# A second norm with two up units on token halves, its chain in a new order, and output products between the last scores

## The chip, the cores and the metric

The kernel runs on one core of a Trainium2 chip. The core has a matrix engine (TensorE, PE in the profile; its weight loads are listed apart as PEld), a vector engine (VectorE, DVE), a scalar engine (ScalarE, ACT), a general engine (GpSimd, POOL) and a synchronising engine (SyncE, SP) that here issues most of the loads. Each engine works through its own instruction list in order; they wait for each other by semaphores. The metric is the time of one execution on the device in microseconds (us); less is better.

## The reference

One decoder layer on 512 tokens of 1024 channels, in float32. The parts that matter here:

```python
# mixer: an mLSTM head group and a convolution group, one output projection
mix = jnp.concatenate([h, y], axis=-1) @ w_out[l]        # (512, 2048) @ (2048, 1024)
x = x + g1 * rms_norm(mix, mix_post_g[l])

# feed-forward with the second norm ahead of it
u = rms_norm(x, ffn_pre_g[l]) * (1.0 + sc2) + sh2
up = causal_dwconv(u @ ffn_up[l], ffn_conv_w[l], ffn_conv_b[l])   # (512, 1024) @ (1024, 5632)
a, gt = jnp.split(up, 2, axis=-1)
f = (jax.nn.silu(gt) * a) @ ffn_down[l]
x = x + g2 * rms_norm(f, ffn_post_g[l])
```

`h` is the output of four mLSTM heads, each with causal scores between positions, done here in 128-position chunks; `y` is the output of the convolution group. `sc2`, `sh2`, `g1` and `g2` come from a conditioning vector through one more projection.

## The kernel before

All large products are done with float32 split in two parts: `w_split` (L185) makes a high part (ScalarE, rounded to the matrix engine's fp32r type) and a low part (source minus high part, on GpSimd unless the caller names VectorE), and `mm3` (L207) adds three products: high x high, high x low, low x high. `w_load` (L195) takes a raw buffer (two in all), issues the load of up to 2048 columns on SyncE, and splits it in four pieces of 512 columns, eight tiles. Split weights lie in a pool of 20 tiles (`wpool`), most other 128x512 tiles in a pool of 36 (`slots`).

The order on TensorE and SyncE is that of the program, written by hand. For the other engines a planner chooses: it walks through a simulated time, and each engine takes from what is ready the instruction that stands first in the program. Within the block `with in_order():` (L75, used from L1026 on) those three engines keep the program's order among the block's own instructions; instructions from outside the block can still be placed between them.

**The last head and the output projection, first half.** `attention(H - 1)` (L536) is a generator: its first two steps are the scores of two chunks each (TensorE, tile `s`, L544, scaled by VectorE, L545), the others the products with the values and the head's norm. Between the steps the program puts `mix_first(n)` (L735): for the n-th of 16 channel groups and all four token tiles (128 tokens each), three products of 512 columns into the four banks `mixa`, which hold the left half of the projection's output. The right half, `mixb`, follows from L936 on: the first 8 channel groups for all four token tiles together, the last 8 per token tile in `mix_last(tt, a, b)` (L994).

**The second norm.** Per token tile of 128 tokens there is a chain of steps:

- `chain_sums` (L955): sum of squares of the tile's `mixb` bank on ScalarE, the product with the gain row `g1r` on VectorE (`un`, L961), and `token_factor` (L714): a tiny VectorE instruction and a power on GpSimd.
- `chain_x` (L964): the new residual `x` (VectorE, L968, two halves of 512 columns), its squares (ScalarE), the product with the row `gs2r` (VectorE, L971), another factor.
- `chain_u` (L974): `un` times the factor plus the row `sh2r` (VectorE, L976).
- `turn_tile` (L980): eight 128x128 transposes on TensorE (`xT`, L984) into two banks of the pair `at`.
- `turn_out` (L986): high part on ScalarE (`u2h`, L991), low part on VectorE (`u2l`, L992).

The results lie in `u2h` and `u2l`, sorted by token half (tiles 0 and 1, tiles 2 and 3). The feed-forward's up projection has 22 units of 256 output channels (two banks each); a unit's weights are one raw block. `up_half(th, i)` (L1012) computes a unit for one token half with products of 256 columns, so it can start when two token tiles are ready. The first `NE = 3` units are done so; from unit 3 on a product takes all 512 columns (L1139). Unit 0's block is split by `w_load` with VectorE for the low parts; units 1 and 2 have their splits (`up_split`, L1005, VectorE for the low parts) at written places in the chain. The rows `gs2r` and `sh2r` go through DRAM: `send_rows` (L682) transposes the gains on TensorE and stores them, `row` (L691) reads them back to all partitions.

Of the kernel before, what the change touches and what calls it, by code (L numbers as in the profile page):

```python
# [20 lines left out]
KT = D // P  # L21
# [34 lines left out]
def decoder_layer(ctx, tc, w_glu0, x, c, adaT, vecs, w_glu, w_qko, w_v0, w_vo, w_out, w_up, w_down, out):  # L56
# [138 lines left out]
    def w_load(view, name, pool=None, tag="w", eng=None):  # L195

        n = view.shape[1]
        r = raws.tile([P, 2048], F32, tag="raw", name=name)
        nc.sync.dma_start(r[:, :n], view)
        return [w_split(r[:, a : min(a + T, n)], f"{name}_{a}", pool, tag, eng) for a in range(0, n, T)]  # L200
# [481 lines left out]
    def send_rows(a, n, queue=nc.scalar):  # L682

        ps = mmbank(f"gT{a}") if a == KT else atbank(f"gT{a}")
        PE.transpose(ps[:n, :P], gains[:, a : a + n], ident)
        t = (side if a == 3 * KT else slot)(f"gTs{a}")[:, :P]
        V.tensor_copy(t[:n, :], ps[:n, :P])
        for i in range(n // KT):
            queue.dma_start(rows_d[a // KT + i].rearrange("(j p) -> j p", p=P), t[i * KT : (i + 1) * KT, :])
# [24 lines left out]
    def token_factor(sq, name):  # L714

        t = small.tile([P, 1], F32, tag="tt", name=f"{name}t")
        last_factor[0] = V.tensor_scalar(out=t, in0=sq[:, :1], scalar1=sq[:, 1:2], scalar2=D * EPS, op0=ALU.add, op1=ALU.add)
        r = small.tile([P, 1], F32, tag="tr", name=f"{name}r")
        G.tensor_tensor(out=r, in0=t, in1=mhalf[:, :1], op=ALU.pow)
        return r  # L720
# [4 lines left out]
    KA = 8  # L725
# [9 lines left out]
    def mix_first(n):  # L735
        if n % 4 == 0:
            wo[0] = wo_rows(0, n // 4)
        k = MIX[n]
        for tt, ps in enumerate(mixa):
            mm3(ps, (hy[k][0][:, tok(tt)], hy[k][1][:, tok(tt)]), wo[0][n % 4], n == 0, n == 2 * KT - 1)  # L740
# [150 lines left out]
    tc.cur_priority -= LATER  # L891
    wo = {}
    steps = attention(H - 1)
    next(steps)
    mix_first(0)
    next(steps)
    tc.cur_priority += LATER
    for i in range(20, 24):
# [3 lines left out]
    tc.cur_priority -= LATER  # L902
    norm_rows()
    norm_tiles(0, 4)
    mix_first(1)
    mix_first(2)
    mix_first(3)
    mix_first(4)
# [46 lines left out]
    def chain_sums(tt):  # L955

        ps = banks[tt]
        sq_sum(ps, msq[:, 2 * tt + 1 : 2 * tt + 2], f"mixb{tt}")
        un = adas.tile([P, D], F32, tag="ada", name=f"un{tt}")
        uns[tt] = [un[:, :T], un[:, T:]]  # L960
        V.tensor_tensor(out=uns[tt][1], in0=ps, in1=g1r[1], op=ALU.mult)  # L961
        return token_factor(msq[:, 2 * tt : 2 * tt + 2], f"rm{tt}")

    def chain_x(tt, r):  # L964

# [8 lines left out]
    def chain_u(tt, r):  # L974
        for hf, un in enumerate(uns[tt]):
            V.scalar_tensor_tensor(out=un, in0=un, scalar=r, in1=sh2r[hf], op0=ALU.mult, op1=ALU.add)  # L976
# [3 lines left out]
    def turn_tile(tt):  # L980
        turned[tt] = [atbank(f"xT{tt}_{hf}") for hf in range(2)]
        for tp, un in zip(turned[tt], uns[tt]):
            for i in range(NT):
                PE.transpose(tp[:, i * P : (i + 1) * P], un[:, i * P : (i + 1) * P], ident)  # L984

    def turn_out(tt):  # L986
        for hf, tp in enumerate(turned[tt]):
            js = slice(NT * hf, NT * (hf + 1))
            part = tp.rearrange("p (j t) -> p j t", j=NT)
            hi, lo = (z[:, tt // 2, js, (tt % 2) * P : (tt % 2 + 1) * P] for z in (u2h, u2l))  # L990
            S.activation(hi, part, AF.Copy)  # L991
            last_lo[0] = V.tensor_tensor(out=lo, in0=part, in1=hi.bitcast(F32), op=ALU.subtract)  # L992

    def mix_last(tt, a, b):  # L994
        for n_, k in enumerate(MIX[KA:]):
            if a <= n_ < b:
                mm3(banks[tt], (hy[k][0][:, tok(tt)], hy[k][1][:, tok(tt)]), wo[n_], False, n_ == 2 * KT - KA - 1)

    def raw_up(i):
        r = raws.tile([P, 2048], F32, tag="raw", name=f"wup{i}")  # L1000
        nc.sync.dma_start(r, w_up[i])
        up_w[i] = []
        return r

    def up_split(i, r, pool, tag):  # L1005
        q = len(up_w[i])
        up_w[i].append(w_split(r[:, q * T : (q + 1) * T], f"wup{i}_{q * T}", pool, tag, V))

    NE = 3
    early = []  # L1010

    def up_half(th, i, only=None):  # L1012
# [4 lines left out]
                mm3(ps[:, th * HT : (th + 1) * HT], blk(up_w[i], half * KT + k), (u2h[:, th, k, :], u2l[:, th, k, :]), k == 0, k == KT - 1)  # L1017

    up_w = {0: w_load(w_up[0], "wup0", slots, "t", V)}
    send_rows(KT, 2 * KT, nc.sync)  # L1020
    gs2r = row(1, cvtile, "gs2", nc.sync)
    sh2r = row(2, cvtile, "sh2", nc.sync)
    raw1 = raw_up(1)
    raw2 = raw_up(2)
    early += [[mmbank(f"up{i}_{half}") for half in range(2)] for i in range(2)]
    with in_order():  # L1026
        for tt in range(3):
            mix_last(tt, 0, 2 * KT - KA)
        r = chain_sums(0)
        r = chain_x(0, r)  # L1030
        up_split(1, raw1, slots, "t")
        chain_u(0, r)
        turn_tile(0)
        mix_last(3, 0, 7)
        r = chain_sums(1)
        up_split(1, raw1, slots, "t")
        r = chain_x(1, r)
        up_split(1, raw1, slots, "t")
        chain_u(1, r)
        turn_out(0)  # L1040
        turn_tile(1)
        mix_last(3, 7, 2 * KT - KA)
        r = chain_sums(2)
        turn_out(1)
        r = chain_x(2, r)
        up_split(1, raw1, slots, "t")
        chain_u(2, r)
        up_half(0, 0)
        turn_tile(2)
        r = chain_sums(3)  # L1050
        up_split(2, raw2, wpool, "w")
        r = chain_x(3, r)
        up_split(2, raw2, wpool, "w")
        chain_u(3, r)
        up_half(0, 1)
        up_split(2, raw2, wpool, "w")
        early.append([cvbank(f"up2_{half}") for half in range(2)])
        up_half(0, 2, 0)
        turn_tile(3)
        turn_out(2)  # L1060
        up_split(2, raw2, wpool, "w")
        turn_out(3)
    up_half(0, 2, 1)
    for i in range(NE):
        up_half(1, i)
    for tt in range(NT):
# [53 lines left out]
    for i in range(NF):  # L1120
        if i < NE:
            pa, pg = early[i]
        else:
            pieces = w_load(w_up[i], f"wup{i}")
            if i in AT:
                weight_load(AT.index(i))
            if i in (4, 8, 12, 16):
                ada_block(38 + i // 2, last_lo[0])
                ada_block(39 + i // 2, last_lo[0])
            if i == 19:  # L1130
                ada_done(40, 48)
                gain(3, 40, "ffn_post_g")
            if i == 20:
                send_rows(3 * KT, KT)
            both = []
            for half in range(2):
                ps = mmbank(f"up{i}_{half}")
                for k in range(KT):
                    mm3(halves(ps), blk(pieces, half * KT + k), (u2h[:, :, k, :], u2l[:, :, k, :]), k == 0, k == KT - 1)  # L1139
                both.append(ps)  # L1140
            pa, pg = both
        a = conv3(pa, i, f"fa{i}")
        g = conv3(pg, NF + i, f"fg{i}")
        anchor[0] = S.activation(g, g, AF.Silu)
        if i % 2 == 0:
            x_, r_, *more = side_parts(f"f{i}") if i >= AT[-1] else [slot(f"f{q}{i}") for q in "xr"]
        cs = slice(i % 2 * HT, (i % 2 + 1) * HT)
        V.tensor_tensor(out=x_[:, cs], in0=a[:, :HT], in1=g[:, :HT], op=ALU.mult)
        V.tensor_tensor(out=r_[:, cs], in0=a[:, HT:], in1=g[:, HT:], op=ALU.mult)
        if i % 2:  # L1150
            y_, q_ = more or [slot(f"f{q}{i}") for q in "yq"]
            G.tensor_tensor(out=y_[:, :HT], in0=r_[:, :HT], in1=r_[:, HT:], op=ALU.add)
            G.tensor_tensor(out=y_[:, HT:], in0=y_[:, :HT], in1=x_[:, :HT], op=ALU.subtract)
            G.tensor_tensor(out=q_[:, :HT], in0=x_[:, :HT], in1=r_[:, :HT], op=ALU.subtract)
            G.tensor_tensor(out=q_[:, HT:], in0=x_[:, HT:], in1=y_[:, HT:], op=ALU.subtract)
            home = [None, None]
            if i == NF - 1:
                ends = [adas.tile([P, D], F32R, tag="ada", name=f"f{q}{i}") for q in "xy"]
                home = [(z[:, :T], z[:, T:]) for z in ends]
            af.append(split_f(x_, f"fx{i}", i == 1, home[0]))  # L1160
            asum.append(split_f(y_, f"fy{i}", i == 1, home[1]))
            j = i // 2
            nc.scalar.dma_start(spill["s34"][:, j * T : (j + 1) * T], q_)
            nc.scalar.dma_start(spill["a22"][:, j * HT : (j + 1) * HT], r_[:, HT:])
        if i - 1 in AT:
            weight_store(AT.index(i - 1))
        if i in AT:
            weight_sums(AT.index(i))
# [196 lines left out]
```

## Time and profile before

| | |
|---|---|
| median of 3 runs | 770.94 us (770.82 to 772.68) |
| the profiled execution | 771.52 us, span 769.8 us |
| granted TensorE clock | 0.998 |
| last head's scores, start of the first | 314.9 us |
| `mix_last` of the right half | 391.4 to 414.8 us |
| first up product | 414.8 us |
| last of the four turnings | 430.7 us |

Times within the profile count from the start of its span, and belong to one execution. A row of the timeline has its start, its length, the engine, the line, the operation, the tiles written and read, and in brackets how long the engine had been idle and what ended that. Where a row stands for several instructions (x2), its length is that of them all. Matrix products overlap; their spacing is the cost, not the length of one. A window's row has the busy time of PE, PEld, DVE, ACT and POOL (instructions in brackets), the clock, the share of the DMA engines and their GB/s.

### The profile page before, as it was taken

To read this page: it belongs to the slowest core of one execution; us is meant where nothing else is said; L and a number is where in the kernel's file an instruction comes from. 1 tells how busy PE (TensorE), PEld (TensorE's weight loads), DVE (VectorE), ACT (ScalarE), POOL (GpSimd) and SP (SyncE) were. 2 spreads that over 40 slices of the span, in tenths; PEclk is the share of its full clock that TensorE was granted. 3 is DMA by queue.
4 is the path that set the end of the run, shared out by engine and by line. 5 is a ranking of instruction groups with operands and counts; after the bars stand their busy time and mean duration, and the time that the engine had idled before them with its cause. 6 is when DMAs were issued, how large, how long until landed. Compare 5 with 4: busy or idle time off the path is not lost.

```text
span 769.8 us, 10292 instructions
## 1 busy us (share of the span) xinstructions
PE 758.5 (99%) x3562; PEld 630.5 (82%) x3562; DVE 573.7 (75%) x831; ACT 408.4 (53%) x780; POOL 522.7 (68%) x432
## 2 busy tenths in 40 slices
PE   8999999999999999999999999999999999999996
PEld 6788898878788788788888998888888888888885
DVE  5669999979979696476949797675765677654548
ACT  7585438585665645573334554434445246566633
POOL 4789759795494871645611467886978786599943
PEclk9999999999999999999999999999999999999999
DMA  8973214311131250655953655856686584896273
GB/s 317 347 277 126 100 56 140 135 54 56 54 111 55 110 181 38 246 192 164 378 193 135 246 185 196 301 213 232 221 302 220 215 294 145 303 399 239 96 242 141
DMA packets 40137, 147.34 MB, mean 191 GB/s; under 512 B 3826, under 2 KB 5266, under 8 KB 30484
## 3 DMA queue, kind: packets, MB, share of 16 engines
q1 hardware_dynamic: 26372, 94.50, 34.1%
q10 hardware_dynamic: 13712, 52.18, 18.8%
q8 instruction: 28, 0.46, 0.2%
q14 instruction: 25, 0.20, 0.1%
HBM read 126.59 MB, written 20.07 MB: 191 GB/s over the span
## 4 chain that ended last, share of the span: by engine, by line
PE 91%; DMA 2%; DVE 2%; POOL 2%; issue 1%; ACT 1%; DVEq 0%; POOLq 0%; ACTq 0%
PE up L210 31%; PE qko L210 13%; PE dn L210 10%; PE vo L210 9%; PE glu L210 7%; PE mixa L210 6%; PE mixb L210 6%; PE s L544 2%; PE o L555 2%; PE glu L356 2%; PE v L210 1%; DMA p<-spill_t 1%; DMA wglu<-in_w_glu 1%; POOL wglu_0l L192 0%; PE cps L159 0%
## 5 line engine op out<-in xcount | busy, mean ns | idle before, releaser
L767 DVE SCALAR_TENSOR_TENSOR cv<-gt,cvw,cv 128x485 f32<-128x485 f32 (+23 forms) x200 | 137.1, 731 | 2.9 <-ACT cv L755 1.3
L763 POOL TENSOR_TENSOR cs<-cs,cs 128x510 f32<-128x510 f32 (+3 forms) x32 | 42.1, 1318 | 0.1
L210 PE MATMUL up<-u2l,wup_0h 128*128 128x512 f32 (+1 forms) x100 | 36.5, 365 | 0.1
L210 PE MATMUL up<-u2h,wup_0h 128*128 128x512 f32 (+1 forms) x100 | 36.5, 365 | 0.0
L210 PE MATMUL up<-u2h,wup_1024h 128*128 128x512 f32 (+1 forms) x100 | 36.4, 364 | 0.0
L210 PE MATMUL up<-u2h,wup_0l 128*128 128x512 f32 (+1 forms) x100 | 36.4, 364 | 0.0
L210 PE MATMUL up<-u2l,wup_512h 128*128 128x512 f32 (+1 forms) x100 | 36.4, 364 | 0.0
L210 PE MATMUL up<-u2h,wup_512h 128*128 128x512 f32 (+1 forms) x100 | 36.4, 364 | 0.0
L210 PE MATMUL up<-u2h,wup_1536h 128*128 128x512 f32 (+1 forms) x100 | 36.4, 364 | 0.0
L210 PE MATMUL up<-u2l,wup_1536h 128*128 128x512 f32 (+1 forms) x100 | 36.4, 364 | 0.0
L210 PE MATMUL up<-u2h,wup_1536l 128*128 128x512 f32 (+1 forms) x100 | 36.4, 364 | 0.0
L210 PE MATMUL up<-u2h,wup_512l 128*128 128x512 f32 (+1 forms) x100 | 36.4, 364 | 0.0
L210 PE MATMUL up<-u2h,wup_1024l 128*128 128x512 f32 (+1 forms) x100 | 36.4, 364 | 0.0
L210 PE MATMUL up<-u2l,wup_1024h 128*128 128x512 f32 (+1 forms) x100 | 36.3, 363 | 0.0
L176 DVE SCALAR_TENSOR_TENSOR junk<-ada,cb 128x1024 bf16<-128x1024 f32 x20 | 30.1, 1506 | 4.9 <-DMA ada<-in_adaT 4.8
L192 POOL TENSOR_TENSOR wup_0l<-wup,wup_0h 128x512 fp32r<-128x512 f32 x19 | 29.3, 1543 | 4.5 <-ACT wup_0h L191 4.5
L192 POOL TENSOR_TENSOR wup_1024l<-wup,wup_1024h 128x512 fp32r<-128x512 f32 x19 | 25.0, 1318 | 9.4 <-ACT wup_1024h L191 9.4
L192 POOL TENSOR_TENSOR wup_1536l<-wup,wup_1536h 128x512 fp32r<-128x512 f32 x19 | 27.6, 1455 | 4.7 <-ACT wup_1536h L191 4.4
L761 ACT ACTIVATE cs<-gt,cvw 128x511 f32<-128x511 f32 (+4 forms) x40 | 27.2, 712 | 6.3 <-POOL cs L763 3.8
L1099 DVE TENSOR_TENSOR b<-b 128x512 f32<-128x512 f32 x11 | 19.4, 1760 | 11.3 <-POOL b L1098 11.3
L1098 POOL TENSOR_TENSOR b<-b 128x512 f32<-128x512 f32 x11 | 14.2, 1291 | 17.3 <-DVE b L1097 17.3
L336 DVE SCALAR_TENSOR_TENSOR junk<-ada,cps 128x1024 bf16<-128x1024 f32 x16 | 19.5, 1219 | 8.3 <-ACT cb L411 4.6
(1097 smaller groups left out, 2738.5 us busy)
## 6 DMA issues: line engine op xcount, KB each, us to landing
wup<-in_w_up SPq DMA_DIRECT2D x22, 1024.0 KB, 6.0
b<-in_w_down ACTq DMA_DIRECT2D x11, 1024.0 KB, 5.1
spill_t<-b ACTq DMA_DIRECT2D x11, 1024.0 KB, 3.9
ada<-in_adaT ACTq DMA_DIRECT2D x20, 512.0 KB, 4.0
wqko<-in_w_qko SPq DMA_DIRECT2D x9, 1024.0 KB, 4.8
ada<-in_adaT SPq DMA_DIRECT2D x16, 512.0 KB, 7.2
wo<-in_w_out SPq DMA_DIRECT2D x8, 1024.0 KB, 4.8
wvo<-in_w_vo SPq DMA_DIRECT2D x6, 1024.0 KB, 4.8
```

What stands on the lines that cost most here:

```text
L176: t = V.scalar_tensor_tensor(out=junk, in0=r, scalar=1.0, in1=cb, op0=ALU.mult, op1=ALU.mult, accum_out=mod[:, i : i + 1])
L192: (eng or G).tensor_tensor(out=lo[:, :n], in0=src, in1=hi[:, :n].bitcast(F32), op=ALU.subtract)
L210: PE.matmul(ps, l, r, start=start and i == 0, stop=stop and i == 2, skip_group_check=again)
L336: V.scalar_tensor_tensor(out=junk, in0=first[k][:, i * D : (i + 1) * D], scalar=1.0, in1=cps, op0=ALU.mult, op1=ALU.mult, accum_out=part[: ...
L356: PE.matmul(ps, blk(wk, i)[a], u[k][b], start=k == 0 and p == 0, stop=k == KT - 1 and p == 1)
L544: PE.matmul(sp[:, :n], ks[d][:, cc * P : (cc + 1) * P], qs[d][:, cc * P :], start=d == 0, stop=d == 1)
L555: PE.matmul(o[:, : DH + 2], E[h][cc][:, a : a + P], vs[h][cc], start=cc == 0, stop=cc == tt)
L761: S.activation(t[:, d:], cvx[j][:, : T - d], AF.Copy, scale=w(CK - 1 - d))
L763: G.tensor_tensor(out=side[:, d:], in0=side[:, d:], in1=t[:, d:], op=ALU.add)
L767: tap = V.scalar_tensor_tensor(out=cp[:, d:], in0=cvx[j][:, : T - d], scalar=w(CK - 1 - d), in1=cp[:, d:], op0=ALU.mult, op1=ALU.add)
L1098: G.tensor_tensor(out=b12, in0=b22, in1=b12, op=ALU.subtract)
L1099: V.tensor_tensor(out=b22, in0=b22, in1=b11, op=ALU.subtract)
```

## The change

Four edits.

1. `mix_first(0)` moves ahead of the last head's first scores, and `mix_first(1)` from behind `norm_tiles(0, 4)` to between the two score steps.
2. In `chain_sums` the factor is made ahead of the product with `g1r`.
3. `NE` goes from 3 to 2: two units are computed on token halves. Unit 2's block is an ordinary `w_load` behind the block, and is computed with 512 columns like the later units. Unit 1's load is issued ahead of the rows' transfers, not behind them.
4. In the chain, three of unit 1's four splits stand ahead of tile 0's sums, and the fourth before `chain_u(0)`. The turnings of tiles 0 to 3 stand after half of tile 2's `mix_last`, after half of tile 3's, between the two halves of unit 0's first token half, and between those of unit 1's. `turn_out(0)` and `turn_out(2)` stand ahead of `chain_u(1)` and `chain_u(3)`, `turn_out(1)` between `chain_x(2)` and `chain_u(2)`.

```diff
@@ -891,8 +891,9 @@
     tc.cur_priority -= LATER
     wo = {}
     steps = attention(H - 1)
+    mix_first(0)
     next(steps)
-    mix_first(0)
+    mix_first(1)
     next(steps)
     tc.cur_priority += LATER
     for i in range(20, 24):
@@ -902,7 +903,6 @@
     tc.cur_priority -= LATER
     norm_rows()
     norm_tiles(0, 4)
-    mix_first(1)
     mix_first(2)
     mix_first(3)
     mix_first(4)
@@ -958,8 +958,9 @@
         sq_sum(ps, msq[:, 2 * tt + 1 : 2 * tt + 2], f"mixb{tt}")
         un = adas.tile([P, D], F32, tag="ada", name=f"un{tt}")
         uns[tt] = [un[:, :T], un[:, T:]]
+        r = token_factor(msq[:, 2 * tt : 2 * tt + 2], f"rm{tt}")
         V.tensor_tensor(out=uns[tt][1], in0=ps, in1=g1r[1], op=ALU.mult)
-        return token_factor(msq[:, 2 * tt : 2 * tt + 2], f"rm{tt}")
+        return r
 
     def chain_x(tt, r):
 
@@ -1006,7 +1007,7 @@
         q = len(up_w[i])
         up_w[i].append(w_split(r[:, q * T : (q + 1) * T], f"wup{i}_{q * T}", pool, tag, V))
 
-    NE = 3
+    NE = 2
     early = []
 
     def up_half(th, i, only=None):
@@ -1017,50 +1018,46 @@
                 mm3(ps[:, th * HT : (th + 1) * HT], blk(up_w[i], half * KT + k), (u2h[:, th, k, :], u2l[:, th, k, :]), k == 0, k == KT - 1)
 
     up_w = {0: w_load(w_up[0], "wup0", slots, "t", V)}
+    raw1 = raw_up(1)
     send_rows(KT, 2 * KT, nc.sync)
     gs2r = row(1, cvtile, "gs2", nc.sync)
     sh2r = row(2, cvtile, "sh2", nc.sync)
-    raw1 = raw_up(1)
-    raw2 = raw_up(2)
     early += [[mmbank(f"up{i}_{half}") for half in range(2)] for i in range(2)]
     with in_order():
-        for tt in range(3):
+        for tt in range(2):
             mix_last(tt, 0, 2 * KT - KA)
+        for _ in range(3):
+            up_split(1, raw1, slots, "t")
         r = chain_sums(0)
         r = chain_x(0, r)
         up_split(1, raw1, slots, "t")
         chain_u(0, r)
+        mix_last(2, 0, 4)
         turn_tile(0)
-        mix_last(3, 0, 7)
+        mix_last(2, 4, 2 * KT - KA)
         r = chain_sums(1)
-        up_split(1, raw1, slots, "t")
         r = chain_x(1, r)
-        up_split(1, raw1, slots, "t")
+        turn_out(0)
         chain_u(1, r)
-        turn_out(0)
+        mix_last(3, 0, 4)
         turn_tile(1)
-        mix_last(3, 7, 2 * KT - KA)
+        mix_last(3, 4, 2 * KT - KA)
         r = chain_sums(2)
+        r = chain_x(2, r)
         turn_out(1)
-        r = chain_x(2, r)
-        up_split(1, raw1, slots, "t")
         chain_u(2, r)
-        up_half(0, 0)
+        up_half(0, 0, 0)
         turn_tile(2)
+        up_half(0, 0, 1)
         r = chain_sums(3)
-        up_split(2, raw2, wpool, "w")
         r = chain_x(3, r)
-        up_split(2, raw2, wpool, "w")
+        turn_out(2)
         chain_u(3, r)
-        up_half(0, 1)
-        up_split(2, raw2, wpool, "w")
-        early.append([cvbank(f"up2_{half}") for half in range(2)])
-        up_half(0, 2, 0)
+        up_half(0, 1, 0)
         turn_tile(3)
-        turn_out(2)
-        up_split(2, raw2, wpool, "w")
         turn_out(3)
-    up_half(0, 2, 1)
+        up_half(0, 1, 1)
+    up_w[2] = w_load(w_up[2], "wup2")
     for i in range(NE):
         up_half(1, i)
     for tt in range(NT):
@@ -1121,7 +1118,7 @@
         if i < NE:
             pa, pg = early[i]
         else:
-            pieces = w_load(w_up[i], f"wup{i}")
+            pieces = up_w.get(i) or w_load(w_up[i], f"wup{i}")
             if i in AT:
                 weight_load(AT.index(i))
             if i in (4, 8, 12, 16):
```

## The prediction

> **What bounds the kernel now.** I read the page's busy times and its chain first.
>
> ```profile
> PE 758.5 (99%) x3562; PEld 630.5 (82%) x3562; DVE 573.7 (75%) x831; ACT 408.4 (53%) x780; POOL 522.7 (68%) x432
> PE 91%; DMA 2%; DVE 2%; POOL 2%; issue 1%; ACT 1%; DVEq 0%; POOLq 0%; ACTq 0%
> ```
>
> TensorE sets the time nearly everywhere, so an edit is worth only the idle time or the products that it takes from PE, and costs whatever makes PE wait. I therefore went to the two places that the diff touches: the last head's scores, and the second norm. For the first, the waits of PE and a window; for the second, the chain in order of time (start, length, engine and tile).
>
> ```profile
> PE s L544 <- DVE hl L593: 0.5, 1, 0.5
> ```
> ```profile
> 312.80:315.60 2.80, 2.35 (x18) 2.03 (x17) 1.51 (x3) 1.92 (x4) 2.80 (x3) 1.00 0.96 367
> ```
> ```profile
> 391.36 16.37 PE mixb L210 x72
> 407.73 0.87 PE xT L984 x8
> 408.60 4.80 PE mixb L210 x21
> 413.40 0.45 PE xT L984 x4
> ...
> 415.26 5.90 PE up L210 x47
> 421.16 0.87 PE xT L984 x8
> 422.03 8.63 PE up L210 x72
> 430.66 0.87 PE xT L984 x8
> 431.53 20.61 PE up L210 x170
> ```
>
> 72 output products (512 columns) take 16.37 us, 0.2274 each; 72 up products on a token half (256 columns) take 8.63, 0.1199 each. The four token tiles are transposed (xT) at 407.73, 413.40, 421.16 and 430.66: PE gives the vector engines 5.7, 7.8 and 9.5 us from one tile to the next. PE waits once here, at the first up product:
>
> ```profile
> 414.60 0.39 PE L210 MATMUL mixb<-wo_1536h,yl 128*128 128x512 f32 x1
> 414.83 0.28 PE L210 MATMUL up<-u2h,wup_0h 128*128 128x256 f32 x1
> 415.26 0.38 PE L210 MATMUL up<-u2l,wup_0h 128*128 128x256 f32 x1
> 415.48 0.28 PE L210 MATMUL up<-u2h,wup_0l 128*128 128x256 f32 x1
> ```
>
> Three products, 0.36 at that rate, should end at 415.19; the fourth comes at 415.60, so 0.41 us is lost on u2l.
>
> **The change, part by part.**
>
> *Scores.* mix_first(0) fills PE's wait before the last head's scores: its banks, weights and left sides (heads 0 and 1) are long ready, and the idle time is 2.80 - 2.35 = 0.45 us of the window above. Bounds 0 and 0.45; I take 0.45. The second score pair, norm_rows and norm_tiles come one mix_first later (12 products, 2.7 us), and their first user, mix_first(6), is four mix_first further on: nothing.
>
> *Two units on halves.* Unit 2 goes from 96 products of 256 columns (11.51 us) to 48 of 512 (10.92): 0.59 gained. [...]
>
> *Order of the chain.* Per token tile VectorE does this (tile 2; the last row is turn_out's):
>
> ```profile
> 413.51 0.68 DVE L961 TENSOR_TENSOR un<-mixb,g1r 128x512 f32<-128x512 f32 x1
> 414.11 0.21 DVE L717 TENSOR_SCALAR rm2t<-msq 128x1 f32<-128x1 f32 x1
> ...
> 415.72 0.74 DVE L968 SCALAR_TENSOR_TENSOR x<-mg,rm2r,x 128x512 f32<-128x512 f32 x1
> 416.38 0.75 DVE L968 SCALAR_TENSOR_TENSOR x<-un,rm2r,x 128x512 f32<-128x512 f32 x1
> 417.04 1.29 DVE L971 TENSOR_TENSOR un<-x,gs2r 128x512 f32<-128x512 f32 x2
> ...
> 419.42 1.41 DVE L976 SCALAR_TENSOR_TENSOR un<-un,rf2r,sh2r 128x512 f32<-128x512 f32 x2
> ...
> 428.21 1.28 DVE L992 TENSOR_TENSOR u2l<-xT,u2h 128x512 fp32r<-128x512 f32 x2
> ```
>
> 0.68 + 2 x 0.21 + 1.49 + 1.29 + 1.41 + 1.28 = 6.6 us by durations (some 0.06 less per instruction by starts: 6.1). After the change PE leaves 24 x 0.2274 + 0.87 = 6.3 us from the first turning to the second, 12 x 0.2274 + 24 x 0.1199 + 0.87 = 6.5 to the third, 48 x 0.1199 + 0.87 = 6.6 to the fourth. So the chain just keeps pace, where it had up to 3 us per tile to spare. The reserve is the one at the first turning: PE gets there at 391.36 + 60 x 0.2274 = 405.0; un of tile 0 starts at 397.66 (row below), and tile 2's way from un to the end of u (413.51 to 420.83, one split and 1.2 us of u2l in it) gives 397.7 + 7.3 - 1.2 = 403.8. That is 1.2; I count 0.9, since three splits now stand ahead of tile 0's sums. The factor put ahead of un lets POOL's power run beside un (up to 0.6 us per tile), which turning inside products uses up: turn_out(1) now stands behind chain_x(2), where it stood ahead of it. If the chain is on time, the 0.41 of the first up product goes; it is 0 otherwise. Undisturbed, the whole change is worth 0.45 + 0.59 + 0.41 = 1.45 us.
>
> *Unit 1's block ahead of the gain rows.* Its buffer comes free when the last output weights are split, and the DMA engines are idle then:
>
> ```profile
> 388.46 1.31 POOL L192 TENSOR_TENSOR wo_1536l<-wo,wo_1536h 128x512 fp32r<-128x512 f32 x1
> ```
> ```profile
> 388.50:392.00 3.50, 3.50 (x18) 2.81 (x17) 2.85 (x4) 2.18 (x4) 1.27 (x2) 1.00 0.00 0
> 402.00:404.00 2.00, 2.00 (x11) 1.65 (x10) 0.48 (x1) 1.15 (x4) 0.55 (x1) 1.00 0.96 369
> ```
> ```profile
> 397.66 0.69 DVE L961 TENSOR_TENSOR un<-mixb,g1r 128x512 f32<-128x512 f32 x1 [5.35 <-ACT mixb0junk L710]
> ```
>
> 1 MB at 369 GB/s is 2.8 us from 389.8, so it should be down before 395 (estimate), and its first three splits are over when tile 0's sum is. The rows queue behind it and come up to 2 us later than now. I cost that at nothing; bound 1.3 us, under rivals.
>
> *Unit 2's block: here the time turns.* It was split by VectorE at written places. Now it is an ordinary w_load: the low halves go to POOL, and the planner is free to place them. It is issued as soon as a raw buffer is free, on SP right behind the rows, and unit 0's buffer is free from 392.1 on:
>
> ```profile
> 391.44 0.68 DVE L192 TENSOR_TENSOR wup_1536l<-wup,wup_1536h 128x512 fp32r<-128x512 f32 x1
> ...
> 418.81 0.69 DVE L192 TENSOR_TENSOR wup_1536l<-wup,wup_1536h 128x512 fp32r<-128x512 f32 x1 [0.31 <-ACT wup_1536h L191]
> ```
> ```profile
> 395.48 0.86 SPq L1001 DMA_DIRECT2D wup<-in_w_up  x2
> 419.53 14.57 SPq L199 DMA_DIRECT2D wup<-in_w_up  x3
> ```
> ```profile
> 427.54 0.62 ACT L191 ACTIVATE wup_0h<-wup 128x512 fp32r<-128x512 f32 x1
> ...
> 431.13 1.09 ACT L991 ACTIVATE u2h<-xT 128x512 fp32r<-128x512 f32 x2 [1.41 <-PE xT L984]
> ```
>
> That is what happened before with unit 3: its buffer freed at 419.5, SP issued it at 419.53, and its splits went ahead of turn_out(3), which stands earlier in the program. So unit 2's block is issued near 397 and lands near 402, and unit 3's (buffer free after unit 1's fourth split) some 5 us later. Of the 20 weight tiles 16 hold the last products' weights: four are free, for two splits at once, and mix_last(3) frees a pair at each of its eight steps, from about 408 to 415. So some eight low halves of units 2 and 3, 1.3 us each, fall on POOL between 403 and 422, where POOL had only the powers. What such a neighbour costs:
>
> ```profile
> L1099 DVE TENSOR_TENSOR b<-b 128x512 f32<-128x512 f32 x11 | 19.4, 1760 | 11.3 <-POOL b L1098 11.3
> ```
> ```profile
> 314.76 0.15 DVE L229 TENSOR_SCALAR ry_t<-ry_s 128x4 f32<-128x4 f32 x1
> ```
> ```profile
> 314.85 1.27 POOL L192 TENSOR_TENSOR wo_1536l<-wo,wo_1536h 128x512 fp32r<-128x512 f32 x1
> 316.08 1.00 POOL L231 TENSOR_TENSOR ry_r<-ry_t,mhalf 128x4 f32<-128x4 f32 x1
> ```
> ```profile
> 428.24 1.30 POOL L192 TENSOR_TENSOR wup_0l<-wup,wup_0h 128x512 fp32r<-128x512 f32 x1 [2.19 <-ACT wup_0h L191]
> ```
>
> A 128x512 subtraction with both inputs in SBUF takes 0.68 alone (391.44) and 1.76 where a POOL split runs: 1.08 lost. A power queues behind a split (ry_t is there at 314.9, POOL takes it at 316.08). But u2l, with one input in PSUM, ran in its usual 1.28 beside POOL's split of 428.24. [...] Of a tile's work, x, gs2r and u have both inputs in SBUF: 1.49 + 1.29 + 1.41 = 4.19 of 6.6, a share of 0.64. Eight splits: 8 x 1.08 x 0.64 = 5.5 us, one power behind half a split 0.6, less the reserve 0.9: PE waits 5.2. From below two splits, 2 x 1.08 x 0.64 - 0.9 = 0.5; from above ten (unit 4's first two as well), each held in full, 10.8 - 0.9 = 9.9. I take 5.2, by the number of buffers that come free.
>
> *Sum.* 0.41 is not gained then: -0.45 - 0.59 + 5.2 = +4.2. The profiled execution took 771.52 (span 769.8), 0.58 above the median 770.94: 775.7 on its scale, **775.1** on the median's.
>
> **The rivals.**
>
> *The chain stays clean* (not slower). The planner puts unit 2's splits behind the chain or into its gaps, so that POOL has only powers until the fourth turning. For it: splits beside un and u2l cost nothing, and the point from which it decides is a late block: were it down after about 417, as unit 3's was, POOL would be too late to harm. Against: nothing on SP holds it back, and everything in these rows starts as soon as it can. 771.52 - 1.45 - 0.58 = 769.5.
>
> *Two splits only.* The two free pairs are used at 403, the rest waits until after the chain: 2 x 1.08 + 0.6 - 0.9 = 1.9, with -1.04: 771.8.
>
> *The rows come late.* Behind 2.8 us of unit 1, gs2r lands after its first use (about 399.5 without the wait): some 1.3 us in front of the first turning, and no collision: 770.94 - 1.04 + 1.3 = 771.2.
>
> **How the numbers follow.** This kernel's measurement can't tell 0.3%, 2.3 us, from no change. Chances: the forecast 0.45 (own range 772.8 to 780), clean 0.32, two splits 0.12, rows 0.08, others 0.03. Clean is the only case that could pass -2.3, by undercutting its sum by 0.9: 0.09 of its 0.32. Same: 0.23 of clean, most of the two small rivals and the forecast's low edge, 0.41. Slower: 0.50. The range 769.0 to 780.0 takes in clean and the upper bound: 771.52 + 9.9 - 1.04 - 0.58 = 779.8.
>
> **What would show it.** Right: splits of wup on POOL between 402 and 422; x and u instructions of 1.3 to 1.9 us; PE waiting at L984 and at the first up product, several us in all. Clean: no POOL split before the fourth turning, up starting within 0.5 us of the last mixb, PE some 1.5 us earlier at unit 3. The scores: no wait at s of the last head. I am wrong if POOL is full of splits there and x still takes 0.7, or if the planner holds them back.

## The result, and the profile after

The changed kernel takes 784.85 us (783.50 to 785.54, 4 runs) against 770.88 for the kernel before in the same rounds: ratio 1.0167, 95% interval [1.0146, 1.0187]. The profiled execution took 785.0, span 783.3. That is 14 us slower, where 775.1 was forecast, and 4.85 above the top of the range. From the page, the busy times and the chain:

```profile
PE 763.2 (97%) x3514; PEld 631.3 (81%) x3514; DVE 578.2 (74%) x827; ACT 410.1 (52%) x780; POOL 526.4 (67%) x436
PE 80%; DMA 6%; POOL 4%; issue 4%; DVE 3%; ACT 2%; SPq 0%; DVEq 0%; ACTq 0%; POOLq 0%
```

PE's share of the chain fell from 91% to 80%, although the kernel issues 48 products fewer. To place the loss I cut the span with three rows of PE's timeline: the last head's transposes, the first `mixb` product, the first `dn` product (of the down projection). Before, then after:

```profile
312.63 1.03 PE L586 MATMUL hT<-ident,hn 128*128 128x128 f32 x8
369.33 0.39 PE L210 MATMUL mixb<-wo_0h,hh 128*128 128x512 f32 x1
658.42 0.39 PE L210 MATMUL dn<-p_0h,fx 128*128 128x512 f32 x1
```
```profile
313.09 1.03 PE L586 MATMUL hT<-ident,hn 128*128 128x128 f32 x8
370.62 0.39 PE L210 MATMUL mixb<-wo_0h,hh 128*128 128x512 f32 x1
671.89 0.39 PE L210 MATMUL dn<-p_0h,fx 128*128 128x512 f32 x1
```

The first stretch holds the edit at the scores: 56.70 became 57.53, **0.83 lost**. The second holds the second norm and the up products: 289.09 became 301.27, **12.2 lost**. These two stretches are used for every run below, because the opening of the kernel moves by up to 3 us from one execution to the next (the last head's transposes start between 310.69 and 313.63). Each comes from one execution. The first repeats well: 57.41 to 57.63 in the nine profiled executions of kernels with the whole of edit 1. The second moves more: the old second norm shows 289.09, 289.11 and 290.29 in three kernels that differ only at the scores. A difference of 1 us in it therefore counts only where rows show what made it. PE's waits at the two places, in the changed kernel (total, times, longest):

```profile
PE xT L985 <- DVE un L962: 3.0, 1, 3.0
PE up L210 <- DVE u2l L993: 2.1, 1, 2.1
PE up L210 <- ACT u2h L992: 1.6, 1, 1.6
PE o L555 <- ACT hn L559: 1.2, 1, 1.2
PE xT L985 <- DVE rm2t L717: 1.1, 1, 1.1
PE xT L985 <- DVE un L977: 0.7, 1, 0.7
```

Five of them, 8.5 us, are in the second norm; the sixth, at `o`, is the new one at the last head. The wait at `s` is gone. First the splits and the vector work that met them, out of the timelines of POOL and of VectorE:

```profile
408.30 1.27 POOL L192 TENSOR_TENSOR wup_0l<-wup,wup_0h 128x512 fp32r<-128x512 f32 x1 [4.93 <-ACT wup_0h L191]
...
428.43 1.73 POOL L192 TENSOR_TENSOR wup_512l<-wup,wup_512h 128x512 fp32r<-128x512 f32 x1
```
```profile
411.33 0.75 DVE L969 SCALAR_TENSOR_TENSOR x<-mg,rm1r,x 128x512 f32<-128x512 f32 x1 [1.69 <-POOL rm1r L719]
...
415.60 2.42 DVE L977 SCALAR_TENSOR_TENSOR un<-un,rf1r,sh2r 128x512 f32<-128x512 f32 x2
...
419.69 1.76 DVE L969 SCALAR_TENSOR_TENSOR x<-mg,rm2r,x 128x512 f32<-128x512 f32 x1 [0.94 <-POOL rm2r L719]
421.37 1.77 DVE L969 SCALAR_TENSOR_TENSOR x<-un,rm2r,x 128x512 f32<-128x512 f32 x1
423.06 3.42 DVE L972 TENSOR_TENSOR un<-x,gs2r 128x512 f32<-128x512 f32 x2
426.53 1.27 DVE L993 TENSOR_TENSOR u2l<-xT,u2h 128x512 fp32r<-128x512 f32 x2
427.73 2.98 DVE L977 SCALAR_TENSOR_TENSOR un<-un,rf2r,sh2r 128x512 f32<-128x512 f32 x2
```

Ten low halves of units 2 to 4 run on POOL between the two rows, among the powers. `x` takes 1.76 where it took 0.74, the product with `gs2r` 3.42 where it took 1.29, `u` 2.42 and 2.98 where it took 1.41; `u2l`, with an input in PSUM, keeps its 1.27. The brackets show the powers standing behind splits. The largest wait is another matter. SyncE, ScalarE and PE:

```profile
397.37 2.37 SPq L695 DMA_DIRECT2D sh2r<-row_d  x2
399.83 26.45 SPq L199 DMA_DIRECT2D wup<-in_w_up  x4
```
```profile
407.59 0.63 ACT L191 ACTIVATE wup_0h<-wup 128x512 fp32r<-128x512 f32 x1 [4.58 <-DMA wup<-in_w_up]
408.13 0.58 ACT L710 ACTIVATE mixb1junk<-mixb 128x512 bf16<-128x512 f32 x1
```
```profile
409.70 0.66 PE L985 MATMUL xT<-ident,un 128*128 128x128 f32 x4 [2.96 <-DVE un L962]
```

ScalarE had the first high part of unit 2 ahead of tile 1's sum of squares, and stood idle 4.58 us for the block, which was issued at 399.83 and reached it only at 407.5. Tile 1's products were over at about 403.4: behind them stand 12 products of tile 2, 0.2274 each, and the first half of the turning at 406.1. So tile 1's factor and its `un` came late. The second half of the first turning writes the bank that this `un` reads, and PE waited 3.0 us for it. Windows of the same stretch (busy PE, PEld, DVE, ACT, POOL, then the granted clock):

```profile
405.00:410.00 5.00, 2.04 (x13) 1.56 (x12) 1.51 (x3) 1.72 (x4) 1.70 (x2) 1.00 0.93 383
...
415.00:420.00 5.00, 3.27 (x15) 2.44 (x14) 4.06 (x7) 2.51 (x7) 3.98 (x4) 0.84 0.01 3
420.00:425.00 5.00, 3.36 (x11) 2.29 (x10) 5.00 (x4) 3.32 (x8) 5.00 (x4) 0.82 0.91 305
425.00:430.00 5.00, 2.92 (x14) 2.74 (x14) 5.00 (x6) 1.85 (x5) 4.25 (x4) 0.52 0.61 216
```

From 420 to 430 VectorE is busy without a gap (5.00 of 5.00 in both windows) and PE is not (3.36 and 2.92): VectorE sets the pace there. The clock falls to 0.52. At the low clock seven output products take 3.1 us from start to start (418.69 to 421.82) and 23 up products 5.1, together 3.9 more than at the usual spacing. Together with the five waits, 8.5, that accounts for the 12.2.

### The profile page after: what moved, and what is told of

It is laid out like the page before. It is cut to its first block, busy times and chain, and to the rows that moved or that the text cites. A ratio compares the mean times of both kernels' runs of the same rounds, so it can differ in the third digit from the quotient of the medians.

```text
span 783.3 us, 10214 instructions
## 1 busy us (share of the span) xinstructions
PE 763.2 (97%) x3514; PEld 631.3 (81%) x3514; DVE 578.2 (74%) x827; ACT 410.1 (52%) x780; POOL 526.4 (67%) x436
## 4 chain that ended last, share of the span: by engine, by line
PE 80%; DMA 6%; POOL 4%; issue 4%; DVE 3%; ACT 2%; SPq 0%; DVEq 0%; ACTq 0%; POOLq 0%
PE up L210 31%; PE qko L210 13%; PE dn L210 9%; PE vo L210 8%; PE glu L210 7%; PE mixa L210 3%; PE o L555 2%; DMA wup<-in_w_up 2%; PE s L544 2%; PE glu L356 2%; PE v L210 1%; DMA wo<-in_w_out 1%; DMA p<-spill_t 1%; DMA wglu<-in_w_glu 1%; POOL wo_1536l L192 1%
## 5 line engine op out<-in xcount | busy, mean ns | idle before, releaser
L192 POOL TENSOR_TENSOR wup_1024l<-wup,wup_1024h 128x512 fp32r<-128x512 f32 x20 | 26.9, 1343 | 23.6 <-ACT wup_1024h L191 23.6
L176 DVE SCALAR_TENSOR_TENSOR junk<-ada,cb 128x1024 bf16<-128x1024 f32 x20 | 28.5, 1424 | 7.4 <-DMA ada<-in_adaT 7.3
L192 POOL TENSOR_TENSOR wup_512l<-wup,wup_512h 128x512 fp32r<-128x512 f32 x20 | 26.7, 1334 | 0.0
```

The lines of the kernel that those rows point to most:

```text
L176: t = V.scalar_tensor_tensor(out=junk, in0=r, scalar=1.0, in1=cb, op0=ALU.mult, op1=ALU.mult, accum_out=mod[:, i : i + 1])
L192: (eng or G).tensor_tensor(out=lo[:, :n], in0=src, in1=hi[:, :n].bitcast(F32), op=ALU.subtract)
```

## The experiments

Theory: the splits of units 2 to 4 do all the harm in the second norm, on two separate ways. ScalarE waits in order for a block, and POOL's low halves hold VectorE and the powers. Rivals: the new order of the chain is itself too tight; the falling clock is a large part; the number of splits matters, not what they read. All kernels named here contain the whole change unless it is said that they start from the kernel before.

**Splits of units 2 to 4 behind the chain.** `behind` puts one instruction of an engine after another one of the same engine.

```diff
+        h = S.activation(hi[:, :n], src, AF.Copy)
+        if hold[0] is not None:
+            behind(h, hold[0])
...
+    hold[0] = last_hi[3]      # the high part of turn_out(3)
     up_w[2] = w_load(w_up[2], "wup2")
```

> The changed kernel, but the high parts of units 2, 3 and 4 stand behind turn_out(3) on ScalarE, so no split of these units (and no wait for their blocks) can stand in the chain. Theory (the splits that the planner puts into the chain are the loss: ScalarE waits for unit 2's block, POOL holds VectorE, the clock falls after PE's waits): no POOL split before the fourth turning, PE waits under 1.5 us in all between 391 us and unit 2, granted clock 0.998, time 770 to 773 us. Rival (the written order itself is too tight: periods of 6.3 to 6.6 us without reserve, turn_out(1) behind chain_x(2)): PE still waits over 4 us at the turnings and the first up product, time above 777 us.

Measured: 770.88, ratio to before 0.9987 [0.9977, 0.9997]; stretches 57.49 and 288.55. PE's waits there and at `o`, two of its products, and POOL's first split:

```profile
PE o L560 <- ACT hn L564: 1.1, 1, 1.1
PE up L215 <- DVE u2l L998: 0.3, 1, 0.3
```
```profile
413.65 0.28 PE L215 MATMUL up<-u2h,wup_0h 128*128 128x256 f32 x1
...
414.55 0.28 PE L215 MATMUL up<-u2h,wup_0h 128*128 128x256 f32 x1
```
```profile
426.01 1.30 POOL L197 TENSOR_TENSOR wup_0l<-wup,wup_0h 128x512 fp32r<-128x512 f32 x1 [5.62 <-ACT wup_0h L194]
```

With nothing changed but the place of the splits, the second stretch falls by 12.7 us (301.27 to 288.55) and comes out 0.5 below the kernel before. The new order is not too tight: all four turnings run without a wait. Only the first up products are late: from the first to the fourth 0.90 us pass, where three take 0.36. This run is the base for the next ones.

**Only the low halves held back**, so that ScalarE's wait for the block remains, and POOL has only powers until the last of them.

```diff
+        l = (eng or G).tensor_tensor(out=lo[:, :n], in0=src, in1=hi[:, :n].bitcast(F32), op=ALU.subtract)
+        if hold[0] is not None:
+            behind(l, hold[0])
...
+    hold[0] = last_pow[0]     # the power of tile 3's second factor
     up_w[2] = w_load(w_up[2], "wup2")
```

> The changed kernel, but only the low halves of units 2, 3 and 4 on POOL are held, behind the last power of the chain; their high parts stay where the planner puts them. Tells POOL's part from ScalarE's wait for the block. Theory: x takes 0.75 us again, the wait at the first turning (3.0 us, ScalarE behind unit 2's block) stays, the waits at the second turning and the first up product go to under 1 us together: 774 to 777 us. If POOL is not the main cause: 781 us or more.

Measured: 774.47, 1.0031 [1.0017, 1.0044]; second stretch 293.39, **4.8 above the base**. One wait, and a window behind it:

```profile
PE xT L990 <- DVE un L967: 3.6, 1, 3.6
```
```profile
410.00:415.00 5.00, 4.07 (x14) 3.36 (x15) 4.61 (x9) 2.45 (x7) 1.08 (x2) 0.71 0.38 147
```

So ScalarE's wait alone costs several microseconds. This profiled execution is the slowest of the six, 3.3 us above their median; by the ratios (1.0031 against 0.9987) it is 3.4. PE's wait is 3.6 of the 4.8. Behind it the granted clock is down to 0.71, and eight products take 3.4 us from start to start (412.15 to 415.53) where eight usually take 1.8, which covers the rest.

**The same high parts behind `turn_out(0)`** instead of `turn_out(3)`: ScalarE's wait is gone, POOL's splits fall into the chain.

```diff
-    hold[0] = last_hi[3]
+    hold[0] = last_hi[0]
```

> The changed kernel, but the high parts of units 2, 3 and 4 stand behind turn_out(0) on ScalarE: by then the block is down, so ScalarE does not wait for it ahead of tile 1's squares, while the splits still run on POOL beside tiles 1 to 3. Theory: the 3.0 us at the first turning go, x of tile 2 still takes 1.76 us, PE still waits 4 to 6 us at the first up product, the clock still falls: 780 to 784 us. If ScalarE's wait is the main cause: below 776 us.

Measured: 779.56, 1.0105 [1.0085, 1.0125]; second stretch 297.44, **8.9 above the base**. No wait at the first turning, one of 0.9 at the second. PE's longer waits, and VectorE's timeline:

```profile
PE up L215 <- ACT u2h L997: 3.3, 1, 3.3
PE up L215 <- DVE u2l L998: 2.1, 1, 2.1
```
```profile
408.23 3.38 DVE L982 SCALAR_TENSOR_TENSOR un<-un,rf1r,sh2r 128x512 f32<-128x512 f32 x2
...
413.28 1.77 DVE L974 SCALAR_TENSOR_TENSOR x<-mg,rm2r,x 128x512 f32<-128x512 f32 x1 [0.95 <-POOL rm2r L724]
414.98 1.75 DVE L974 SCALAR_TENSOR_TENSOR x<-un,rm2r,x 128x512 f32<-128x512 f32 x1
416.65 3.42 DVE L977 TENSOR_TENSOR un<-x,gs2r 128x512 f32<-128x512 f32 x2
...
421.73 3.46 DVE L982 SCALAR_TENSOR_TENSOR un<-un,rf2r,sh2r 128x512 f32<-128x512 f32 x2 [0.35 <-POOL rf2r L724]
```

Against 1.41, 0.75, 0.75, 1.29 and 1.41 in the undisturbed chain these rows lost 1.97 + 1.02 + 1.00 + 2.13 + 2.05 = 8.2 us, and the powers 1.3 more. Ten splits run on POOL here too. Both ways together would make 4.8 + 8.9 = 13.7, and the changed kernel shows 12.7; by the ratios it is 3.4 + 9.1 = 12.5 against 13.9. So the two ways make up the loss to within about 1 us. Whether they overlap isn't shown.

**POOL just as busy, but reading nothing.** As the last kernel, with the low halves of units 2 to 4 left out: POOL writes zeros three times into each low tile, so these units are computed with zero low parts.

```diff
         if hold[0] is not None:
             behind(h, hold[0])
+        if hold[0] is not None:
+            for _ in range(3):
+                G.memset(lo[:, :n].bitcast(F32), 0.0)
+            return hi, lo
```

> The kernel with the high parts of units 2 to 4 behind turn_out(0), but the low halves of these three units are left out: in place of each POOL writes zeros three times (0.5 us each), so POOL is as long in use and reads nothing from SBUF. The output lacks these low halves. Tells the common SBUF way of POOL and VectorE from POOL's own queue. Theory (it is the two readers: each low half holds an x, gs2r or u instruction): x takes 0.75 us, u 1.4 us for two, PE's waits from the second turning on fall from 6.3 to under 2 us, 771 to 775 us. Rival (powers late behind POOL's other work): x starts late but is as short, waits stay over 4 us, 777 us or more.

Measured: 774.33, 1.0045 [1.0026, 1.0064]; second stretch 291.82, 3.3 above the base, not 8.9. PE's waits from the second turning on are 2.4 in all, a little over the 2 expected, against 6.3 in the last kernel. One write on POOL, and `x` and `u` beside such writes:

```profile
412.33 0.53 POOL L199 MEMSET wup_1024l<- 128x512 f32 x1
```
```profile
411.49 0.75 DVE L978 SCALAR_TENSOR_TENSOR x<-mg,rm2r,x 128x512 f32<-128x512 f32 x1 [0.95 <-POOL rm2r L728]
...
418.56 1.41 DVE L986 SCALAR_TENSOR_TENSOR un<-un,rf2r,sh2r 128x512 f32<-128x512 f32 x2 [2.11 <-POOL rf2r L728]
```

VectorE's instructions keep their lengths beside writes (`x` 0.75, `u` 1.41, where splits made them 1.77 and 3.46 in the last kernel); only the powers come late. So 5.6 of the 8.9 (4.6 by the ratios) come with what a split reads, and the queue for the powers can do 3.3 by itself, though writes and splits do not stand in quite the same order. By what way a split that reads holds VectorE, no run here shows.

**The clock.** The changed kernel with transposes of the identity into a bank not yet in use (24 and 15 at the first two turnings, 30 before the first up product), which keep PE busy where it waited.

```diff
+        for _ in range(n):
+            PE.transpose(early[1][1][:, 3 * P :], ident, ident)
```

> The changed kernel with transposes of the identity into a bank that is not yet in use (24 in the middle of the first turning, 6 and 9 at the second, 30 ahead of the first up product, 0.11 us each), placed where PE waits: PE has work while it waits, nothing else is changed. Theory (the clock falls because PE was idle; some 4 us of the loss are products at a lower clock): granted clock 0.998, the 23 up products behind the first wait take 2.8 us, not 5.1, time 780 to 782 us. Rival (the lower clock has another cause, or its price is small): clock stays near 0.991, time 784 us or more.

Measured: 783.24, 1.0154 [1.0137, 1.0171], between the forecast and the rival. It was run once more beside the changed kernel on one chip:

> The changed kernel once more, on the same chip as the filled one, to price the clock: theory of the fallen clock 1 to 2 us above the filled kernel; if the lower clock costs nothing, the same time within its interval.

> The changed kernel with transposes where PE waits, once more beside the changed kernel itself: granted clock 0.998 or more; 1 to 2 us below the changed kernel if the clock's price is real; the same if the vector chain sets PE's pace anyway.

Measured there: 785.09, 1.0172 [1.0144, 1.0201] unfilled and 782.74, 1.0150 [1.0117, 1.0183] filled; second stretch 300.55 and 299.16 (301.27 and 300.10 in the pair of the first runs). A window of the filled kernel (the second of its executions) and two rows of its VectorE:

```profile
425.00:430.00 5.00, 4.83 (x42) 4.62 (x41) 4.88 (x6) 0.84 (x3) 4.18 (x4) 1.00 0.44 151
```
```profile
416.06 1.76 DVE L969 SCALAR_TENSOR_TENSOR x<-mg,rm2r,x 128x512 f32<-128x512 f32 x1
...
428.01 1.76 DVE L969 SCALAR_TENSOR_TENSOR x<-mg,rm3r,x 128x512 f32<-128x512 f32 x1
```

The clock stays at 1.00, where the changed kernel's window shows 0.52, so it had fallen because PE was idle. Yet only 1.2 to 1.4 us of the stretch come back, of the 3.9 that the slow products took (2.35 by the medians of the last pair). The intervals of the two ratios overlap; the two pairs agree in sign. `x` of tile 2 still takes 1.76, and now tile 3's does too, which took 0.75 in the changed kernel; PE waits 1.5 us at the fourth turning, where it had not waited. While VectorE paces the stretch, a faster PE only waits longer. So the filled kernel is not the changed kernel at a full clock: 1.2 to 1.4 is what the filling brings, and the price of the clock by itself stays open.

**Edit 1 alone, on the kernel before.**

```diff
     steps = attention(H - 1)
+    mix_first(0)
     next(steps)
-    mix_first(0)
+    mix_first(1)
     next(steps)
...
     norm_tiles(0, 4)
-    mix_first(1)
```

> The kernel before with only the first edit: mix_first(0) ahead of the last head's scores, mix_first(1) between them. Theory: 0.45 to 0.6 us are gained at the scores, but norm_rows and the projection blocks behind them come 2.3 us later, a load issue on ScalarE waits there for VectorE, hn of the last head is late and PE waits 1.0 to 1.3 us at the products with the values (o): 0.5 to 1 us slower than before (ratio 1.0005 to 1.0015). Rival (my forecast's own step: a gain of 0.45, nothing lost): ratio 0.9994, no wait at o.

Measured: 772.75 against 772.23, 1.0007 [0.9993, 1.0020], no difference by the ratio. The stretches say more: 57.54 for the first, 0.84 above the kernel before and equal to the changed kernel's 57.53 within 0.01. The wait at `s` is gone, and a new one stands at `o`. It is 1.2 us long, as in the changed kernel, whose timeline of ScalarE shows its origin:

```profile
338.32 0.33 ACTq L174 DMA_DIRECT2D ada<-in_adaT  x1
338.70 0.66 ACT L559 ACTIVATE hn<-o 128x256 f32<-128x256 f32 x2 [1.02 <-DVE junk L176]
```

ScalarE also issues loads of `ada`. One of these needs a buffer that VectorE frees with `junk`, and with the second score pair further back the `junk` products are later too. The load stood ahead of `hn` on ScalarE and held it; the next `o` product waited for `hn`. The second stretch of this run is the 290.29: unit 1's block is split 1.3 us later than in the kernel before, counted from the first `mixb` product, and PE waits 1.0 us at tile 1's turning. The old chain, too, hangs on when a block lands.

**The same idle time filled without moving the second score pair**: `mix_first(0)` ahead of both score steps, `mix_first(1)` where it was, on the kernel before.

```diff
     steps = attention(H - 1)
+    mix_first(0)
     next(steps)
-    mix_first(0)
     next(steps)
```

> The kernel before, but mix_first(0) ahead of both score steps, which follow each other; mix_first(1) stays behind norm_tiles. The idle time before the scores is filled, norm_rows comes 0.5 us earlier, not 2.3 us later. Theory: no wait at o, 0.3 to 0.6 us faster (ratio 0.9993). Rival: the two score steps side by side wait for their banks (VectorE reads the first), and it is no faster.

Measured: 771.79, 0.9992 [0.9979, 1.0006]: inconclusive as a ratio. The first stretch is 56.14, 0.56 below the kernel before, and PE waits neither at `s` nor at `o`.

**The changed kernel with the splits behind the chain and this order of scores.**

```diff
+    hold[0] = last_hi[3]
     up_w[2] = w_load(w_up[2], "wup2")
...
     mix_first(0)
     next(steps)
-    mix_first(1)
     next(steps)
...
     norm_tiles(0, 4)
+    mix_first(1)
```

> The changed kernel with both repairs: the splits of units 2 to 4 held behind turn_out(3), and mix_first(0) ahead of both score steps with mix_first(1) in its old place. Theory: the wait at o goes and with it 1.1 us against the kernel with the held splits alone: 769 to 770 us, ratio to before 0.997 to 0.998. Rival: with the chain free of splits, the scores cost nothing any more, and it is the same as with the held splits alone (0.9987).

Measured: 770.71 against 772.23, 0.9979 [0.9969, 0.9990]; stretches 56.13 and 289.06. It is faster than both kernels, by 1.5 us against the one before. The second norm here gains nothing on it (289.09): the first up products lose 1.0 us in this execution, 0.54 in the base. So its gain beyond the 0.57 at the scores isn't located in these stretches.

**POOL instead of VectorE in the old chain.** On the kernel before, unit 2's four low halves stay at their written places, but go to POOL.

```diff
-        up_w[i].append(w_split(..., pool, tag, V))
+        up_w[i].append(w_split(..., pool, tag, eng))     # eng = G for unit 2
```

> The kernel before, unit 2's four splits at their written places in the chain (tiles 3's sums to turn_out(3)), but with the low halves on POOL in place of VectorE. The old order has 2 to 3 us of reserve per tile there. Theory (a split on POOL costs only where the chain has no reserve): each low half holds an x or u instruction for up to 1.1 us, PE waits less than 0.5 us more, time within 0.2% of before. Rival (a POOL split in the chain costs its price anywhere): 4 x 1.08 x 0.64 = 2.8 us, 774 us or more.

Measured: 773.35, 1.0006 [0.9992, 1.0020]; second stretch 290.07, 1.0 above before. VectorE, out of its timeline:

```profile
423.39 1.77 DVE L968 SCALAR_TENSOR_TENSOR x<-mg,rm3r,x 128x512 f32<-128x512 f32 x1 [0.72 <-POOL rm3r L719]
...
427.92 3.48 DVE L976 SCALAR_TENSOR_TENSOR un<-un,rf3r,sh2r 128x512 f32<-128x512 f32 x2 [0.72 <-POOL rf3r L719]
```

The hold is there in full, 1.02 and 2.07 us, but only three splits meet such an instruction, and this chain has time to spare. Of PE's 1.0 some 0.3 are lost at tile 1's turning, ahead of the first of these splits; the fourth turning comes 0.45 later on top. That is the "less than 0.5" that was expected, far from the rival's 2.8.

## Why the prediction was wrong in size

The direction, the place and the named mechanism held. The sum was +4.2 and came to +13.0 in the two stretches: +0.8 at the scores where -0.45 stood, about -0.5 for unit 2 and the order of the chain where -0.59 stood, +8.9 for the splits on POOL where +5.2 stood, +4.8 for ScalarE's wait where nothing stood, less the 1.0 by which the last two exceed the whole. So two steps failed most: ScalarE's wait for the block was put at nothing, and the splits on POOL and the powers behind them were counted too low. Step by step:

- **Scores, "I take 0.45" and "nothing".** The wait at `s` went, as said. The step that failed is "norm_rows and norm_tiles come one mix_first later ... nothing". It looked at the first user on PE and not at the other queue that hangs on the later scores, VectorE's `junk` and behind it ScalarE's load. Measured +0.84 with this edit alone, -0.56 with the order that leaves the second pair in place.
- **Unit 2 on 512 columns, 0.59, and the chain that "just keeps pace".** With the splits held the turnings wait for nothing. What failed is the 0.41 that should go "if the chain is on time". It is on time, and by the spacing that gave 0.41 the first up products lose 0.54 in the base (0.90 - 0.36) and 1.0 in the held run with the other order of scores. `turn_out(1)` now stands behind `chain_x(2)`, and in the base the chain to the first up product goes from tile 2's `x` over its squares on ScalarE to `u2h` and `u2l`. So the stretch gained 0.5 in the one run and 0.0 in the other, of 1.0 predicted. Without these losses it is 288.68 before and 288.01 and 288.05 in the two: the 0.59 is there. The reserve of 0.9 was about right: tile 0's `u` ends 0.5 us ahead of the first turning in the base, 1.1 in the run with the high parts behind `turn_out(0)`.
- **Unit 1's block ahead of the rows, "nothing", bound 1.3.** The block came at 396.2, not before 395. VectorE waited 0.55 us for `sh2r`, inside the bound, and the first turning still began without a wait:

```profile
404.95 0.75 DVE L977 SCALAR_TENSOR_TENSOR un<-un,rf0r,sh2r 128x512 f32<-128x512 f32 x1 [0.55 <-DMA sh2r<-row_d]
```

- **Unit 2's block, the splits on POOL: 5.5 + 0.6 - 0.9 = 5.2.** Mechanism right, size off. The price of 1.08 held (`x` 1.76 - 0.75 = 1.01, `gs2r` 1.07 for each half). The count was ten, not eight; the planner reached unit 4, which the text had only in its upper bound. And the powers behind splits cost 1.69 + 0.94 = 2.6, not 0.6. The share of splits that hold something, 0.64, was about right: the rows of the changed kernel lost 1.01 + 1.01 + 1.02 + 2.13 + 1.57 = 6.7, which is 6.7 / (10 x 1.08) = 0.62. With these terms the step gives 6.7 + 2.6 - 0.9 = 8.4. In the third experiment the parts differ (8.2, a share of 0.76, and 1.3 for the powers), and the step gives 8.6, against 8.9 measured.
- **The missing term: ScalarE in order.** This is the step that was put at nothing. "Lands ~402" was 407.5 (the two transfers of `sh2r` held SyncE until 399.7, and the block then took 7.7 us: 1 MB at 137 GB/s, while the window from 405 to 410 has 383 GB/s in all). I priced the arrival only for POOL. A late arrival was even my case for a clean chain, "were it down after about 417". But the high part is ScalarE's, the planner had put it ahead of tile 1's squares, and there it blocks until the block is down. Alone it costs 4.8 in the profiled execution, 3.4 by the ratios. By itself it would have brought 775.1 to 779.9, just inside the range; with the 3.7 that the splits cost beyond their 5.2, and the scores, the result is outside.
- **The clock.** Not in the sum. It falls (0.52 to 0.84), and the products that it slows take 3.9 us more; filling PE's waits gave back 1.2 to 1.4.

Of the rivals, the clean chain (769.5, or 1.45 below the kernel before) is about what the same change gives when the splits are kept behind the chain (770.88 against 771.60, and 770.71 against 772.23 with the other order of scores); nothing in the kernel kept them there. Two splits only, and late rows without a collision, did not happen.

## What to carry to other kernels

A step that is handed to a planner needs a price on every engine that it issues to, and for each of them the question of what stands behind it in order if its data comes late. When weights are prepared beside a tight chain, put that work behind the chain by an explicit order, as the held runs do. An engine whose reads don't meet those of the chain might serve as well; no run here tries one. Judge a reordering by the stretch that it touches, since two opposite effects of half a microsecond can't be seen in 770, and by the rows in it, since a stretch of the same code can move by 1 us.

## What was not expected of the hardware

The granted clock gave way to waits of a few microseconds in a kernel that had 0.998 before, and stayed low after work came back. Behind waits of 1.6 and 2.1 us, with one product between them, the chain of the changed kernel and PE's timeline show

```profile
427.26 5.13 PE up L210 x23
```
```profile
428.50 0.41 PE L210 MATMUL up<-u2h,wup_0h 128*128 128x256 f32 x1
428.71 0.41 PE L210 MATMUL up<-u2l,wup_0h 128*128 128x256 f32 x1
```

that is 0.223 us for each up product and 0.21 from one start to the next, where it was 0.1199. The granted clock is 0.52 in the window from 425 to 430, and 0.79 from 430 to 435, where PE is busy throughout (5.00); from 435 to 440 it is 1.00 again. A wait of 2.96 us at 406.7 had not done that: the windows from 405 to 410 and from 410 to 415 show 1.00. Why that longer wait left the clock alone and the two shorter ones did not, no run here shows.

The other surprise is the price of a load issued from an engine that also computes: 0.33 us of issue held ScalarE 1.02 us, because it waited for a buffer.
